# A planned decoder step on one core: samples' attention outputs taken by transposes and address patterns, value products in two row ranges, other planner constants

## The chip, the cores and the metric

The kernel runs on one core of a Trainium2 chip. The metric is the device time of one execution in microseconds. Three timed executions of the kernel before took 797.78, 797.87 and 798.31 us; their median is 797.87 us.

The core has five queues that run side by side: TensorE (PE in the profile; its weight loads are PEld), VectorE (DVE), ScalarE (ACT), GpSimd (POOL) and SyncE (SP), which here only issues transfers. Products land in PSUM, whose banks hold 512 float32 columns on 128 partitions; VectorE and ScalarE read them from there.

## The reference

One layer of a decoder computes a prompt of 512 tokens (`SEQ`) and 32 sample tokens (8 samples of 4 tokens, `NB`, `TS`, `NS`) with shared weights, all in float32. Cut to what matters here:

```python
h = rmsnorm(x, norm_mix)
z = h @ w_in                                  # aq, ak, av for 8 heads of 64; hq, hf, hi, hg for 4 heads of 128
att = dilated_attention(aq, k_all, v_all, q_idx)      # samples: k_all, v_all = cached window + new rows
att = head_rmsnorm(att, att_out_norm)
o, s_new = hgrn2_recurrence(...)
x = x + jnp.concatenate([att, o], axis=-1) @ w_out
c = rmsnorm(x, norm_cross)
cq = (c @ w_cq).reshape(B, T, X_H, X_DH)      # 4 heads of 128
s = jnp.einsum('bthd,bmhd->bhtm', cq, mem_k) * X_DH ** -0.5
co = jnp.einsum('bhtm,bmhd->bthd', softmax(s), mem_v)
x = x + co.reshape(B, T, X_W) @ w_co
x = x + (silu(conv(rmsnorm(x) @ w_gate)) * (rmsnorm(x) @ w_up)) @ w_down
```

For a sample, both attentions sum value rows that belong to that sample alone: the window attention over the cached rows and the four new tokens, the cross attention over 256 memory rows.

## The kernel before

Activations stand with features on the partitions (128 at a time) and the 544 tokens along the free dimension; the last 32 columns are the samples. Every large weight product is made of three products of split operands (`h` and `l` tiles: the rounded part, written by ScalarE, and the rest, written by VectorE). The input projection, the output projection `ps_wo`, the cross projections `ps_cq` and `ps_co`, and the feed-forward part (`ps_ag` to `ps_du`, then `ps_dz` and its like) follow one another. The samples' attention runs beside them.

**How samples are attended.** The scores of a sample need a query per head, so the queries are laid out as 32 columns per sample (8 heads x 4 tokens), each with zeros outside its own head. Four samples fill 128 rows of a score tile: row 32 b + 4 h + t belongs to sample b of the group, head h and token t. There are two such groups, `g` = 0 and 1. `decode_attention` computes the scores against the streamed key tiles (`psd`), applies the softmax, turns the probabilities by transposes (`psdt`), and multiplies them with the streamed value rows into `psdo`. That product makes for each of the 128 rows all 512 value features; a row of head h needs only the 64 features of its own head.

**How each row's own features are picked before.** `own_blocks` multiplies the product with `1 / den` (`dden`) and with a 0/1 mask `h8`, which zeroes the features of the other heads. `decode_finish` adds what the new tokens bring: per group four products of 32 x 32 probabilities (`pnew`) with the 32 new value rows (`vnew`), into `psdn`, masked in the same way (`domn`) and added to the masked `dom`. Then eight products with the 0/1 matrix `sel8` (128 x 16) sum over the heads' rows and at the same time turn the tile, so that features stand on partitions (`psds`). One copy takes that to `attS`, which is normalised, scaled and split into the tiles `am0h` to `am3l` that `ps_wo` reads. `cross_sample` does the same for cross attention with the mask `h4` (four heads of 128), the matrix `sel4`, and `ps_cos`, which `split_psum` turns into the last 32 columns of `coh` and `col`, read by the second halves of `ps_co`.

The new value rows come from `prompt_attention`: for each of four pairs of heads `by_token_s` multiplies the 32 sample columns of v with the identity into a spare corner of a score bank (32 rows x 128 columns), and a copy takes them to `vnew`.

**What sets the order.** The whole program is recorded first and put into an order by a planner, the class `Tape`. A call on an engine becomes a `Step`; neighbouring calls of one engine become one step (`tape.cut()` ends it). TensorE steps recorded inside `tape.main()` are *mains* and keep their order; all else is a *side*. `due` gives every side a time by which it should begin, worked back from the mains that use its result (`MARGIN` ahead of a main, `SLACK` where nothing presses). `order` then runs a simple model of the engines with a guessed length for each call and starts at every free engine the ready step that is due first, at most `LEAD` ahead of its time. For TensorE it collects ready sides until their lengths sum to `BURST`, or `PATIENCE` has gone by, or one is overdue, and then plays them in a run; a side of another array shape is put back by `NEAR`, and `SWITCH` is the modelled cost of a change of shape. `ACTIVE` and `SPELL` hold sides back that would leave too little matmul work in a spell of time. `run` first spreads the mains evenly over the total length of TensorE's steps, plans, moves each main's estimate 0.3 of the way to its planned start, and plans again, `ROUNDS` times; the plan with the earliest modelled end is issued. So every engine's program, the DMA queues' too, comes out of this plan; line 718 of the profile is where all recorded calls but the transfers (line 690) are issued.

Of the kernel before, what the change touches and what calls it, by code (L numbers as in the profile page):

```python
# [17 lines left out]
SEQ = 512  # L18
# [77 lines left out]
for _n, _c in (("ident", 128), ("ones", 128), ("blk64", 128), ("dbias", NR + 2 * NS),  # L96
               ("mask_a", 96), ("mask_b", 96), ("mask_s", 96), ("batch", 4), ("h8", 8), ("h4", 4), ("sel8", 16),
               ("sel4", 16), ("sel32", 32), ("own", 2)):
    _span(CST_COLS, _n, _c)
# [17 lines left out]
def _constants():  # L117
# [39 lines left out]
    put("h8", (h[:, None] == np.arange(8)[None, :]).astype(np.float32))  # L157
    put("h4", (h[:, None] == np.arange(4)[None, :]).astype(np.float32))
    bt = (p // 32) * TS + t
    put("sel8", (bt[:, None] == np.arange(16)[None, :]).astype(np.float32))  # L160
    put("sel32", (p[:, None] % 32 == np.arange(32)[None, :]).astype(np.float32))
    put("own", ((p[:, None] % 32) // TS == 4 * np.arange(2)[None, :] + p[:, None] // 32).astype(np.float32))
    put("sel4", ((bt[:, None] == np.arange(16)[None, :]) & (h[:, None] < 4)).astype(np.float32))
# [112 lines left out]
class Tape:  # L276
# [7 lines left out]
    ROUNDS = 6  # L284
    BLOCK, AHEAD_OF, FETCH = 256, 63, 4.3
    SWITCH, NEAR = 0.14, 3.0
    SPELL, ACTIVE, IDLE, COLD = 3.4, 0.47, 0.45, 2.0
    BURST, PATIENCE, SLACK, LEAD, MARGIN = 2.0, 4.0, 12.0, 15.0, 4.0
# [152 lines left out]
    def run(self):  # L441

        scale = sum(s.length for s in self.steps if s.engine == "PE") / sum(s.length for s in self.mains)
# [226 lines left out]
class _Engine:  # L670
# [5 lines left out]
    def __getattr__(self, method):  # L676
# [3 lines left out]
        def take(*args, **kw):  # L680
# [10 lines left out]
            if engine == "PE":  # L691
# [6 lines left out]
                else:  # L698
                    least = 0.112 if m == 128 and k == 128 else 0.0105
                    length = 2 * max(least, 0.00086 * n * (max(m, 128 - 2 * k) / 128 if m < 128 else 1.0) * (0.59 if k <= 64 else 1.0))  # L700
                work = n * (1 if method != "transpose" and args[1].dtype == F32R else codes) / 2400.0 * m * k / 16384
# [21 lines left out]
def tile_decoder_step(ctx: ExitStack, tc: tile.TileContext, xT, memT, kwT, vw, s0, conv_in, mkT, mv, vecs, cst,  # L723
# [497 lines left out]
    vnew, vnew_in = tape.tile(strm, [NS, 512], F32, name="vnew"), []  # L1221
# [18 lines left out]
    def decode_attention():  # L1240
# [36 lines left out]
        for g in range(2):  # L1277
            s = dec_p[g]
            pts = []
            for half in range(2):  # L1280
                pt = A(f"dpt{g}{half}")
                ps = PX(f"psdt{g}{half}")
                for c in range(4):
# [3 lines left out]
                    else:  # L1287
                        nc.tensor.transpose(ps[:NS, 128 * c:128 * c + 128], s[:, NR:NR + NS], C("ident"))
                if half == 0:
                    nc.scalar.copy(pt[:, :512], ps)  # L1290
                else:
                    nc.scalar.copy(pt[:, :384], ps[:, :384])
                    nc.scalar.copy(pt[:NS, 384:512], ps[:NS, 384:512])
# [11 lines left out]
            own_blocks(om_old[g], po, g)  # L1305
            nc.vector.tensor_copy(pnew[g], pts[1][:NS, 384:512])
# [5 lines left out]
    pnew = [tape.tile(strm, [NS, 128], F32, name=f"pnew{g}") for g in range(2)]  # L1312
# [3 lines left out]
    def own_blocks(out, ps, g):  # L1316
# [1513 lines left out]
```

## Time and profile before

| what | us |
|---|---|
| median of three timed executions | 797.87 |
| span of the profiled execution, first to last instruction | 796.6 |
| TensorE busy, matmuls | 784.4 (98%) |
| VectorE busy | 674.9 (85%) |
| ScalarE busy | 481.0 (60%) |
| GpSimd busy | 200.6 (25%) |
| TensorE busy, weight loads (beside matmuls) | 743.1 (93%) |

The profiled execution has no device time of its own beside the span; the timed executions lie 1.2 to 1.7 us above the span. Matmuls overlap in the records (a matmul starts before the one ahead of it ends), so what a group costs is the distance between its first start and the first start behind it. One float32 product makes two matmul records, a split product of two `h` or `l` tiles one, and a transpose one. The form `128*32` means 128 rows and 32 columns of the array.

### The profile page before, as it was taken

The page shows a single profiled execution, that of the slowest core. Times are in us where ns is not written, and L with a number is a line of the kernel's source. Part 1 is how long each engine was busy: PE and PEld are TensorE (multiplying, and loading weights), DVE is VectorE, ACT ScalarE, POOL GpSimd, SP SyncE. Part 2 cuts the span into 40 slices and gives each one's busy share as a digit, 9 for nine tenths or more (in the row PEclk, how much of TensorE's full clock was granted, in tenths as well). Part 3 has the DMA queues.
Part 4 walks back from the last instruction along what each step waited for, and adds up shares of the span by engine and source line. Part 5 has one row for each costly group of instructions (what it writes and reads, how often), then busy time and mean ns, then how long its engine had stood idle before and what let it go on. Part 6 is the DMA issues. An engine that isn't in the chain of part 4 may idle for free.

```text
span 796.6 us, 19239 instructions
## 1 busy us (share of the span) xinstructions
PE 784.4 (98%) x7448; PEld 743.1 (93%) x7448; DVE 674.9 (85%) x1515; ACT 481.0 (60%) x1031; POOL 200.6 (25%) x284
## 2 busy tenths in 40 slices
PE   9999999999999999999999999999999999999995
PEld 8999878988888989999999999999999999999994
DVE  6899888587979996674888999999998998979973
ACT  7734468726558535553666678666766666668642
POOL 1130000020220200231234346423533352332023
PEclk9999999999999999999999999999999999999998
DMA  8845795798932455450853368879788878776203
GB/s 303 264 147 163 249 337 191 246 357 286 296 109 80 135 173 196 132 173 26 255 156 95 91 171 193 167 189 205 165 175 206 198 150 208 186 202 168 78 1 112
DMA packets 107419, 144.14 MB, mean 181 GB/s; under 512 B 7360, under 2 KB 73920, under 8 KB 107328
## 3 DMA queue, kind: packets, MB, share of 16 engines
q1 hardware_dynamic: 91728, 124.04, 48.6%
q0 software_dynamic: 14880, 18.36, 15.1%
q8 instruction: 58, 0.95, 0.5%
q10 hardware_dynamic: 720, 0.53, 0.2%
q14 instruction: 33, 0.27, 0.1%
HBM read 134.82 MB, written 8.07 MB: 179 GB/s over the span
## 4 chain that ended last, share of the span: by engine, by line
PE 96%; ACT 1%; DMA 1%; DVE 0%; issue 0%; SPq 0%; DVEq 0%; ACTq 0%
PE ps_ag L718 7%; PE ps_au L718 7%; PE ps_wo L718 6%; PE ps_aw L718 5%; PE ps_cu L718 4%; PE ps_cg L718 4%; PE ps_q L718 3%; PE ps_co L718 3%; PE ps_cq L718 3%; PE ps_dz L718 3%; PE ps_az L718 3%; PE ps_hv L718 2%; PE ps_cw L718 2%; PE ps_first L718 2%; PE ps_ck L718 2%; PE ps_dg L718 2%
## 5 line engine op out<-in xcount | busy, mean ns | idle before, releaser
L718 DVE TENSOR_TENSOR wl<-wr,wh 128x512 fp32r<-128x512 f32 x98 | 70.8, 743 | 0.4 <-ACT wh L718 0.4
L718 ACT CAST wh<-wr 128x512 fp32r<-128x512 f32 x98 | 56.2, 616 | 15.2 <-PE psdo L718 6.0
L718 POOL TENSOR_TENSOR hG<-hG,hf 128x256 f32<-128x256 f32 (+1 forms) x28 | 23.8, 851 | 133.9 <-DVE hf L718 79.7
L718 POOL COPY last<-ug 128x2 f32<-128x2 f32 (+1 forms) x44 | 30.4, 726 | 85.2 <-DVE ug L718 79.3
L718 DVE SCALAR_TENSOR_TENSOR cv<-ug,vec,cv 128x560 f32<-128x560 f32 x44 | 35.1, 797 | 2.6 <-ACT cv L718 2.2
L718 POOL TENSOR_TENSOR acc_cx<-acc_cx,sq_cx 128x256 f32<-128x256 f32 (+1 forms) x14 | 12.3, 879 | 63.4 <-PE ps_wo L718 36.7
L718 ACT ACTIVATE cv<-cv 128x560 f32<-128x560 f32 x22 | 14.8, 672 | 13.4 <-DVE cv L718 13.3
L718 ACT ACTIVATE cv<-ug,vec 128x560 f32<-128x560 f32 x22 | 18.8, 856 | 4.6 <-DVE ug L718 2.1
L718 POOL COPY ug<-conv_state 128x16 f32<-128x16 f32 x22 | 20.7, 945 | 0.1
L718 ACT ACTIVATE P<-P,mx 128x128 f32<-128x128 f32 (+3 forms) x32 | 17.6, 552 | 4.0 <-DVE mx L718 3.8
L690 POOL DMA_DIRECT2D S13w<-in_w_down x12 | 12.2, 1019 | 30.7 <-PE ps_cw L718 15.8
L718 PE MATMUL ps_co<-coh,wh 128*128 128x256 f32 (+1 forms) x64 | 19.0, 297 | 0.0
L718 PE MATMUL ps_co<-col,wh 128*128 128x256 f32 (+1 forms) x64 | 18.4, 288 | 0.0
L718 PE MATMUL ps_co<-coh,wl 128*128 128x256 f32 (+1 forms) x64 | 18.4, 287 | 0.0
L718 DVE TENSOR_TENSOR xr<-xr,ps_wo 128x256 f32<-128x256 f32 (+1 forms) x16 | 6.8, 435 | 13.0 <-PE ps_wo L718 12.9
L718 ACT COPY keptg<-ps_ag 128x272 f32<-128x272 f32 x20 | 7.7, 387 | 15.7 <-PE ps_ag L718 15.7
L718 POOL TENSOR_TENSOR acc_final<-acc_final,sq_final 128x256 f32<-128x256 f32 (+1 forms) x10 | 8.5, 859 | 34.1 <-ACT sq_final L718 20.5
L718 DVE TENSOR_TENSOR xr<-xr,ps_aw 128x272 f32<-128x272 f32 x36 | 15.5, 431 | 0.6 <-PE ps_aw L718 0.6
L718 DVE CUSTOM_DVE_ANT_0 P<-psS,bias 128x128 f32<-128x128 f32 (+3 forms) x32 | 14.1, 486 | 1.9 <-PE psS L718 1.8
L718 PE MATMUL psd<-st,qbd_win 128*32 128x224 f32 x256 | 15.5, 357 | 0.0
L718 PE MATMUL psdo<-st,dpt 128*32 128x256 f32 x224 | 15.3, 384 | 0.0
L718 POOL TENSOR_TENSOR acc_ux<-acc_ux,sq_ux 128x256 f32<-128x256 f32 (+1 forms) x13 | 10.9, 839 | 16.4 <-ACT sq_ux L718 16.4
(3348 smaller groups left out, 3785.6 us busy)
## 6 DMA issues: line engine op xcount, KB each, us to landing
st<-in_kwT SPq DMA_DIRECT2D x32, 448.0 KB, 5.6
st<-in_vw SPq DMA_DIRECT2D x28, 512.0 KB, 6.2
wr<-in_w_in SPq DMA_DIRECT2D x25, 512.0 KB, 6.0
wrg<-in_w_gate SPq DMA_DIRECT2D x10, 512.0 KB, 6.4
wru<-in_w_up SPq DMA_DIRECT2D x10, 512.0 KB, 5.8
st<-in_mkT SPq DMA_DIRECT2D x8, 512.0 KB, 6.2
wr<-in_w_out SPq DMA_DIRECT2D x8, 512.0 KB, 4.5
S13w<-in_w_down SPq DMA_DIRECT2D x24, 128.0 KB, 3.5
```

Of the source, the lines that this page charges most:

```text
L690: return tape.put(engine, lambda: call(*args, **kw), outs, ins, 0.1, 0.3, size)
L718: return tape.put(engine, lambda: call(*args, **kw), outs, ins, length, lag, size, port, codes, work, mode)
```

## The change

1. The masks `h8`, `h4` and the matrices `sel8`, `sel4` are gone from the constants. `psdo` is taken to `dom` by ScalarE with the scale `dden`, unmasked; `ps_cso` to `com` by a plain ScalarE copy.
2. `by_feature` turns a whole 128 x 512 tile by four transposes, and `own_columns` is an address pattern over the result that reads, for head h, sample b and token t, column 32 b + 4 h + t of the block in which head h's features lie. ScalarE copies by that pattern: for the window attention one copy per group and half of the partitions (64 features per head), to `attS`; for cross attention one per group, to a new tile `cos`, from which `split_psum` reads.
3. `pnew` is one tile of 64 rows and `vnew` has 64 rows, with the new value rows twice (`by_token_s` runs for both row ranges). Group 1's products use rows 32 to 63. The last score block of group 1 is transposed as 64 columns, so that its 32 new columns land in rows 32 to 63, and ScalarE writes them to `pnew` directly. The products of both groups are recorded one after another; then comes for each group one VectorE pass (`psdn` times `dden` plus `dom`), a cut, the transposes and the copies.
4. The planner: other values, a factor `EVEN` on the first spread of the mains, two rounds instead of six, and half the modelled length for products of at most 32 rows and 32 columns.

```diff
-    ROUNDS = 6
+    ROUNDS, EVEN = 2, 1.013
     BLOCK, AHEAD_OF, FETCH = 256, 63, 4.3
-    SWITCH, NEAR = 0.14, 3.0
-    SPELL, ACTIVE, IDLE, COLD = 3.4, 0.47, 0.45, 2.0
-    BURST, PATIENCE, SLACK, LEAD, MARGIN = 2.0, 4.0, 12.0, 15.0, 4.0
+    SWITCH, NEAR = 0.14, 3.9
+    SPELL, ACTIVE, IDLE, COLD = 3.4, 0.45, 0.45, 2.0
+    BURST, PATIENCE, SLACK, LEAD, MARGIN = 1.75, 3.7, 16.5, 15.95, 4.95
...
-        scale = sum(s.length for s in self.steps if s.engine == "PE") / sum(s.length for s in self.mains)
+        scale = self.EVEN * sum(s.length for s in self.steps if s.engine == "PE") / sum(s.length for s in self.mains)
...
+                    length *= 0.5 if k <= 32 and m <= 32 else 1.0
...
-    vnew, vnew_in = tape.tile(strm, [NS, 512], F32, name="vnew"), []
+    vnew, vnew_in = tape.tile(strm, [2 * NS, 512], F32, name="vnew"), []
...
-                        nc.tensor.transpose(ps[:NS, 128 * c:128 * c + 128], s[:, NR:NR + NS], C("ident"))
+                        nc.tensor.transpose(ps[:NS + NS * g, 128 * c:128 * c + 128], s[:, NR - NS * g:NR + NS], C("ident"))
...
-                    nc.scalar.copy(pt[:NS, 384:512], ps[:NS, 384:512])
+                    nc.scalar.copy(pnew[own, :], ps[own, 384:512])
...
-            own_blocks(om_old[g], po, g)
-            nc.vector.tensor_copy(pnew[g], pts[1][:NS, 384:512])
+            nc.scalar.activation(om_old[g][:, :512], po, AF.Copy, scale=dden[g])
...
+    def new_rows(g):
+        return slice(NS * g, NS * g + NS)
+
+    def own_columns(ps, rows, first, step, count):
+
+        of = ps[rows, :]
+        return bass.AP(of.tensor, of.offset + first, [list(of.ap[0]), [128 + step, count], [32, 4], [1, TS]])
+
+    def by_feature(om, name):
+
+        ps = PX(name)
+        for c in range(4):
+            nc.tensor.transpose(ps[:, 128 * c:128 * c + 128], om[:, 128 * c:128 * c + 128], C("ident"))
+        return ps
 
     def decode_finish(out):
 
-        oms = []
+        pos = [(PX if g else PDEC)(f"psdn{g}") for g in range(2)]
         for g in range(2):
-            po = (PX if g else PDEC)(f"psdn{g}")
+            rows = new_rows(g)
             for b in range(4):
-                nc.tensor.matmul(po[32 * b:32 * b + 32, :], pnew[g][:, 32 * b:32 * b + 32], vnew, start=True, stop=True)
+                nc.tensor.matmul(pos[g][32 * b:32 * b + 32, :], pnew[rows, 32 * b:32 * b + 32], vnew[rows, :],
+                                 start=True, stop=True)
+        for g in range(2):
             om = A(f"domn{g}")
-            own_blocks(om, po, g)
-            nc.vector.tensor_tensor(om[:, :512], om[:, :512], om_old[g][:, :512], op=ALU.add)
-            oms.append(om)
-        px = PX("psds")
-        for g in range(2):
-            for p in range(4):
-                at = slice(32 * p + 16 * g, 32 * p + 16 * g + 16)
-                nc.tensor.matmul(px[:, at], oms[g][:, 128 * p:128 * p + 128], C("sel8"), start=True, stop=True)
-        nc.scalar.copy(attS, px[:, :128].rearrange("p (q n) -> p q n", q=4))
+            nc.vector.scalar_tensor_tensor(om[:, :512], pos[g], dden[g], om_old[g][:, :512], op0=ALU.mult, op1=ALU.add)
+            tape.cut()
+            px = by_feature(om, f"psds{g}")
+            for hh in range(2):
+                rows = slice(64 * hh, 64 * hh + 64)
+                nc.scalar.copy(attS[rows, :, 16 * g:16 * g + 16].rearrange("p q (b t) -> p q b t", t=TS),
+                               own_columns(px, rows, 4 * hh, 8, 4))
...
-                spare = S[group, 1][:NS, 384:512]
-                by_token_s(v, spare)
+                spare = S[group, 1][:2 * NS, 384:512]
+                for g in range(2):
+                    by_token_s(v, spare[new_rows(g), :])
...
-            nc.vector.tensor_tensor(om[:, :512].rearrange("p (h d) -> p h d", h=4),
-                                    po.rearrange("p (h d) -> p h d", h=4),
-                                    C("h4")[:, :, None].to_broadcast([128, 4, 128]), op=ALU.mult)
+            nc.scalar.copy(om[:, :512], po)
             oms.append(om)
-        pcs = PX("ps_cos")
+        cos = A("cos")[:, :128].rearrange("p (h n) -> p h n", h=XH)
         for g in range(2):
-            for h in range(XH):
-                at = 32 * h + 16 * g
-                nc.tensor.matmul(pcs[:, at:at + 16], oms[g][:, 128 * h:128 * h + 128], C("sel4"), start=True,
-                                 stop=True)
+            pcs = by_feature(oms[g], f"ps_cos{g}")
+            nc.scalar.copy(cos[:, :, 16 * g:16 * g + 16].rearrange("p h (b t) -> p h b t", t=TS),
+                           own_columns(pcs, slice(0, 128), 0, 4, XH))
         for h in range(XH):
-            split_psum(h, pcs[:, 32 * h:32 * h + 32], SEQ, N)
+            split_psum(h, cos[:, h, :], SEQ, N)
```

More of the change, by code (lines that the diff above doesn't have):

```diff
@@ L96 @@
 for _n, _c in (("ident", 128), ("ones", 128), ("blk64", 128), ("dbias", NR + 2 * NS),
-               ("mask_a", 96), ("mask_b", 96), ("mask_s", 96), ("batch", 4), ("h8", 8), ("h4", 4), ("sel8", 16),
-               ("sel4", 16), ("sel32", 32), ("own", 2)):
+               ("mask_a", 96), ("mask_b", 96), ("mask_s", 96), ("batch", 4), ("sel32", 32), ("own", 2)):
     _span(CST_COLS, _n, _c)
@@ L156, in _constants @@
     put("batch", ((p[:64, None] % 32 // TS) == 4 * (p[:64, None] // 32) + np.arange(4)[None, :]).astype(np.float32))
[L157 to L160, printed above, removed]
     put("sel32", (p[:, None] % 32 == np.arange(32)[None, :]).astype(np.float32))
     put("own", ((p[:, None] % 32) // TS == 4 * np.arange(2)[None, :] + p[:, None] // 32).astype(np.float32))
-    put("sel4", ((bt[:, None] == np.arange(16)[None, :]) & (h[:, None] < 4)).astype(np.float32))
     return c
@@ L1291, in decode_attention @@
                 else:
+                    own = new_rows(g)
                     nc.scalar.copy(pt[:, :384], ps[:, :384])
-                    nc.scalar.copy(pt[:NS, 384:512], ps[:NS, 384:512])
+                    nc.scalar.copy(pnew[own, :], ps[own, 384:512])
                 pts.append(pt)
@@ L1311, in tile_decoder_step @@
     om_old = [A(f"dom{g}") for g in range(2)]
-    pnew = [tape.tile(strm, [NS, 128], F32, name=f"pnew{g}") for g in range(2)]
+    pnew = tape.tile(strm, [2 * NS, 128], F32, name="pnew")
     dden = [tape.tile(strm, [128, 1], F32, name=f"drec{g}") for g in range(2)]
     attS = tape.tile(strm, [128, 4, NS], F32, name="attS")
-    def own_blocks(out, ps, g):
-        nc.vector.scalar_tensor_tensor(out[:, :512].rearrange("p (h d) -> p h d", h=8),
-                                       ps.rearrange("p (h d) -> p h d", h=8), dden[g],
-                                       C("h8")[:, :, None].to_broadcast([128, 8, 64]), op0=ALU.mult, op1=ALU.mult)
+    def new_rows(g):
+        return slice(NS * g, NS * g + NS)
```

## The prediction

> **What bounds the kernel now.** I read the page first: the engine totals and the chain that ended last.
>
> ```profile
> span 796.6 us, 19239 instructions
> ...
> PE 784.4 (98%) x7448; PEld 743.1 (93%) x7448; DVE 674.9 (85%) x1515; ACT 481.0 (60%) x1031; POOL 200.6 (25%) x284
> ...
> PE 96%; ACT 1%; DMA 1%; DVE 0%; issue 0%; SPq 0%; DVEq 0%; ACTq 0%
> ```
>
> TensorE is busy for 784.4 of 796.6 us and 96% of the last-ending chain runs through it. A busy share can hide gaps, so next come the busy times by stage, and then what TensorE waited for between the start and the end (9 to 787 us). Columns of the first: the stretch, its length, TensorE's busy time and matmuls, granted clock, DMA share, GB/s.
>
> ```profile
> 160.00:306.30 146.30, 146.30 (x1876) 1.00 0.64 206
> 430.00:730.00 300.00, 299.07 (x2383) 1.00 0.76 178
> 787.00:796.60 9.60, 0.70 (x2) 0.63 0.53 177
> ```
>
> ```profile
> PE ps_au L718 <- ACT keptu L718: 0.9, 1, 0.9
> PE ps_ak L718 <- ACT keptk L718: 0.5, 1, 0.5
> ```
>
> The stretch that holds the samples' attention (160 to 306 us) has no idle time on TensorE, and 300 us of feed-forward work have 0.9. In the middle only two waits are listed, 1.4 us together. So a matmul stream's microsecond is a microsecond of the kernel until something else ends last, and work taken from VectorE or ScalarE alone buys nothing. I cost the change by the time that it takes from or adds to TensorE's stream, from one start to the next (durations overlap, starts do not).
>
> **The change part by part.** *Selection by a mask product becomes selection by address.* Before, two groups of eight 128x16 products with the 0/1 matrices sel8 and sel4 pick each sample's own rows; after, two sets of four 128x128 transposes do it per place, and ScalarE reads only the wanted columns. The TensorE timeline shows both products and, as nearest row for the new form, four transposes between dense matmuls (start, duration, operation).
>
> ```profile
> 296.19 1.86 PE L718 MATMUL psds<-cs,domn 128*128 128x16 f32 x16
> 297.89 0.38 PE L718 MATMUL psr_hg<-hsh,sums 128*128 128x288 f32 x1
> ...
> 411.04 1.85 PE L718 MATMUL ps_cos<-cs,com 128*128 128x16 f32 x16
> 412.74 0.36 PE L718 MATMUL ps_co<-coh,wh 128*128 128x256 f32 x1
> 412.94 0.28 PE L718 MATMUL ps_co<-col,wh 128*128 128x256 f32 x1
> ...
> 379.77 0.60 PE L718 MATMUL ps_cpt<-cs,cp 128*128 128x128 f32 x4
> 380.12 0.36 PE L718 MATMUL ps_cpo<-cpth,mvh 128*128 128x256 f32 x1
> 380.32 0.28 PE L718 MATMUL ps_cpo<-cptl,mvh 128*128 128x256 f32 x1
> 380.44 0.28 PE L718 MATMUL ps_cpo<-cpth,mvl 128*128 128x256 f32 x1
> ...
> 283.95 0.60 PE L718 MATMUL pst_hk<-cs,hk 128*128 128x128 f32 x4
> 284.48 0.41 PE L718 MATMUL psL<-kq 128*32 128x32 f32 x13
> ```
>
> Each product holds TensorE 1.70 us (297.89 - 296.19; 412.74 - 411.04): sixteen records for eight matmuls. Four transposes hold it 0.35 us (380.12 - 379.77). The first dense matmul behind either takes 0.20 instead of 0.12 (380.32 - 380.12 against 380.44 - 380.32; 412.94 - 412.74 is 0.20 too), so splitting a place into two sets costs 0.08 once more. After: 2 x 0.35 + 0.08 = 0.78 per place, saving 1.70 - 0.78 = 0.92, twice, 1.84 us. Bounds: a set that is followed by another array shape holds it 0.53 (284.48 - 283.95); were all four sets so placed, a place would save 1.70 - 1.06 = 0.64, 1.3 in all. Eight transposes in one set save the 0.08 at most.
>
> *New tokens' value products in two row ranges.* pnew and vnew get 64 rows, and the second group of samples works in rows 32 to 63, so that its four 32x32 products can run beside those of the first; both groups become one step.
>
> ```profile
> 276.13 1.06 PE L718 MATMUL psdn<-vnew,pnew 32*32 32x512 f32 x8
> 277.13 1.09 PE L718 MATMUL psO<-PT,vt 128*64 128x128 f32 x16
> ...
> 285.67 1.06 PE L718 MATMUL psdn<-vnew,pnew 32*32 32x512 f32 x8
> 286.66 1.16 PE L718 MATMUL psU<-hvt,hkt 128*128 128x128 f32 x8
> ...
> 288.33 1.13 PE L718 MATMUL psu<-hvm,hsm 32*128 32x512 f32 x4
> 289.38 0.50 PE L718 MATMUL ps_cv<-wh,mmh 128*128 128x512 f32 x1
> ```
>
> Today the two groups hold TensorE 1.00 and 0.99 us, each alone. That row groups overlap here is seen in psu: two 32-row products of 512 columns, in different row groups, take 1.05 us together, as long as four column groups of psdn. I take 1.05 for all eight: saving 1.99 - 1.05 = 0.94. If the second group's first pass starts only with the first group's second pass, they take about 1.5 and save 0.5; with no overlap 0. I take the first, since psu is the nearest row.
> The Trainium skill ("TensorE: Matmul & The Clock Gate", Part 3, what overlaps) says that matmuls start and end strictly in program order; if each product's two passes stood next to each other in that order, the halfway case would hold, 0.44 us less gain. psu's 1.05 us speaks against it, since one such product after another would show more.
>
> *By-token copies of the new values.* by_token_s runs twice, into rows 0 to 31 and 32 to 63, four times in all. The nearest row has two such products of hv side by side:
>
> ```profile
> 275.79 0.41 PE L718 MATMUL psA<-cs,hv 128*32 128x128 f32 x4
> ```
>
> Four records hold TensorE 0.34 us (276.13 - 275.79), about three 0.11 steps for two products; were the added one free, two records would take about the same. I charge 0.03 each, 0.1 in all; were they serial, four pairs of 0.11 passes, 0.9.
> Sum on TensorE: 1.84 + 0.94 - 0.1 = **2.7 us less**, between 0.4 (1.3 + 0 - 0.9) and 2.8.
>
> *VectorE and ScalarE.* The groups by form (busy us, mean ns of one), and from the timeline the one small copy of today:
>
> ```profile
> L718 DVE SCALAR_TENSOR_TENSOR dom<-psdo,drec,cs 128x512 f32<-128x512 f32 x2 | 1.5, 746 | 0.9 <-PE ps_hg L718 0.9
> L718 DVE TENSOR_TENSOR com<-ps_cso,cs 128x512 f32<-128x512 f32 x2 | 1.4, 688 | 0.0
> L718 DVE TENSOR_TENSOR domn<-domn,dom 128x512 f32<-128x512 f32 x2 | 1.3, 686 | 0.0
> L718 ACT ACTIVATE P<-P,den 128x512 f32<-128x512 f32 x4 | 2.8, 721 | 2.1 <-DVE den L718 2.1
> L718 ACT COPY dpt<-psdt 128x512 f32<-128x512 f32 x2 | 1.2, 581 | 0.0
> ...
> 298.08 0.27 ACT L718 COPY attS<-psds 128x128 f32<-128x128 f32 x1 [2.49 <-PE psds L718]
> ```
>
> VectorE loses dom, com and one of the two domn passes, 1.5 + 1.4 + 1.3 = 4.2 us, and two small pnew copies. ScalarE gains two scaled evacuations (nearest: 721 ns), two plain ones (581 ns), and five more small strided copies; at 0.27 us each, as today's attS copy (0.58, the 512-column copy, would be the most), about 1.4 + 1.2 + 1.4 = 4.0 us. Both lie beside TensorE work and I cost them at nothing. The cover is the dense work behind the two places:
>
> ```profile
> 303.42 0.25 DVE L718 SCALAR_TENSOR_TENSOR am3l<-attS,vec,am3h 128x32 fp32r<-128x32 f32 x1
> 307.16 0.28 PE L718 MATMUL ps_wo<-am0h,wh 128*128 128x256 f32 x1
> ...
> 413.50 0.47 DVE L718 TENSOR_TENSOR col<-ps_cos,coh 128x32 fp32r<-128x32 f32 x4
> 415.66 0.30 PE L718 MATMUL ps_co<-coh,wh 128*128 128x288 f32 x1
> ```
>
> attS's last part is ready at 303.67 and the output projection first reads an attention tile at 307.16: 3.5 us of slack, against three more small copies, 0.9. The cross path ends at 413.97 and its first reader starts at 415.66: 1.7 of slack, against two copies in a row, 0.6, less the 0.9 that TensorE needs less. If that cover went, the excess would be paid one for one; next late would be the second half of ps_co. Behind a new ScalarE evacuation that waits on psdo or ps_cso stand the wh casts for the next weights, which have a reader on VectorE (wl) before TensorE needs them; I see no stall of theirs on TensorE now. The constants h8, h4, sel8, sel4 leave the held table (44 columns), one load a little smaller: nothing. g = 1 transposes 64 columns instead of 32 of the last score block, the same instruction count: nothing.
>
> *Other constants of the recorder.* They change the order on all five queues, the loads on SP and POOL included, and two rounds of planning instead of six are compared. Matmul work does not change, so only waits and changes of array shape can move. The two waits above, 1.4 us, may go or double. A step between dense and small shapes costs about the 0.2 seen between a set and its neighbours; ten visits more or fewer, a choice of mine, are +-2 us. I see no sign either way and take 0, with bounds of -2.5 and +4.
>
> The sum is made against this execution, 796.6 of span: 796.6 - 2.7 = 793.9. Timed runs have a median of 797.87, 1.3 above the span, which is what lies around it; I keep that offset: 797.87 - 2.7 = **795.2 us**.
>
> **The rivals.** *The order gains too* (793.0): both waits go (1.4) and some four small-shape visits fewer (0.8): 795.2 - 2.2. For it: the wait for keptu is a queue effect; its copy starts at 726.05 behind other ScalarE work. Against it: no stage but these has idle time.
>
> ```profile
> 726.05 0.36 ACT L718 COPY keptu<-ps_au 128x272 f32<-128x272 f32 x1
> ```
>
> *The packing does not do what it says* (796.9): row groups run one after another (0.94 lost) and the doubled by_token_s is serial (0.8 lost): 795.2 + 1.7, no measurable change. psu and psA speak against it. *A clock window falls.* In the row 787 to 796.6 the clock is 0.63 where TensorE idles; a wait long enough would do that inside. Were 4 us of matmuls, a length that I choose, to run at 0.63, they would take 4 / 0.63 = 6.3: 795.2 + 2.3 = 797.5, still no measurable change. The stretch with most transposes now has 1.00.
> The Trainium skill ("TensorE: Matmul & The Clock Gate", Part 4) says that transposes do not count as activity for the clock; by that, the added transposes would feed this rival. The 1.00 in the stretch 160 to 306, which holds long sets of them, does not bear it out.
>
> *Slower: the feed-forward stream begins to wait for VectorE* (800.5).
>
> ```profile
> 457.50:560.00 102.50, 102.50 (x820) 102.50 (x819) 99.27 (x204) 70.51 (x146) 43.19 (x60) 1.00 0.79 184
> 560.00:650.00 90.00, 90.00 (x721) 90.00 (x721) 87.04 (x187) 58.00 (x121) 37.44 (x53) 1.00 0.83 184
> ```
>
> The third busy time is VectorE's: 99.27 of 102.50 and 87.04 of 90.00, 6.2 us free in all. New leads and margins order its casts anew; where a ready step is put behind one that waits, that reserve is used up, and each late evacuation then stops TensorE for about the 0.9 of keptu. Six such stops cost 5.3: 797.9 - 2.7 + 5.3. It decides from 4.3 us on (five stops). Against it: VectorE's load there does not change, and in 192 us TensorE never waited.
>
> **How the numbers follow.** A measurement tells some 0.2% (1.6 us) from no change: faster means under 796.3, slower over 799.5. The sum alone, 795.2 with 794.0 to 796.3 around it, 0.47; the order gains too 0.21; packing fails or the order takes the gain back, 0.17; clock 0.04; slower 0.11. Faster 0.68, same 0.21, slower 0.11. The range reaches from the order's bound (795.2 - 2.5) to the lower part of the slow case: 792.6 to 798.6.
>
> **What would show it.** psds and ps_cos as four transposes of 0.35 us each; psdn as one run of sixteen records in about 1.05 us; by_token_s pairs starting within 0.02 us; TensorE's busy time near 781.7 with the same few waits; clock 1.00 up to 787. Wrong would be: psdn near 2 us, waits of TensorE on VectorE or ScalarE summing to over 3 us between 430 and 730, a clock row under 1.00, or a first ps_wo or second-half ps_co that waits for attS or cos.

## The result and the profile after

The changed kernel is slower than the kernel before by a little: 799.49 us (median of 21 runs, 798.74 to 801.85) against 798.34 (21 runs, 797.73 to 799.63), a ratio of 1.0016 with a 95% interval of 1.0010 to 1.0023. Run again (e4 below) it gave 1.0017 (1.0008 to 1.0026). The prediction of 795.2, range 792.6 to 798.6, missed the time and the sign.

The page of the changed kernel gives its engine totals and the shares of the chain that ended last.

```profile
span 797.0 us, 19226 instructions
...
PE 784.1 (98%) x7440; PEld 742.0 (93%) x7440; DVE 673.9 (85%) x1507; ACT 480.1 (60%) x1040; POOL 206.6 (26%) x284
...
PE 97%; ACT 1%; DVE 1%; issue 0%; DVEq 0%; ACTq 0%
```

TensorE's busy time is 0.3 lower than before (784.4), where 2.7 were expected. So most of what is missing is not idle time: TensorE is busy longer with the products that did not change. The stretches of the changed kernel (length, TensorE's busy time and matmuls, granted clock, DMA share, GB/s) and TensorE's waits between 9 and 787 us follow.

```profile
160.00:306.90 146.90, 146.06 (x1870) 1.00 0.63 205
430.00:730.00 300.00, 299.02 (x2380) 1.00 0.75 179
```

```profile
PE ps_au L713 <- ACT keptu L713: 0.9, 1, 0.9
PE psds L713 <- ACT ho L713: 0.7, 1, 0.7
PE ps_ak L713 <- ACT keptk L713: 0.5, 1, 0.5
PE psA L713 <- issue: 0.2, 1, 0.2
```

The attention stretch, 146.3 of 146.3 busy before, now has 0.84 idle in 146.9, and of that 0.67 is one wait: the new transposes into psds wait for ScalarE's copy into ho. The clock is 1.00 in both. Next the rows of the changed products on TensorE (start, duration, operation).

```profile
275.28 1.09 PE L713 MATMUL psdn<-vnew,pnew 32*32 32x512 f32 x16
276.30 1.53 PE L713 MATMUL psO<-PT,vt 128*64 128x128 f32 x24
...
295.29 0.66 PE L713 MATMUL psds<-cs,domn 128*128 128x128 f32 x4 [0.67 <-ACT ho L713]
295.88 0.40 PE L713 MATMUL psin<-hsm 32*128 32x32 f32 x2
...
296.68 0.63 PE L713 MATMUL psds<-cs,domn 128*128 128x128 f32 x4
297.07 0.48 PE L713 MATMUL ps_cv<-wh,mmh 128*128 128x512 f32 x1
...
410.16 1.03 PE L713 MATMUL ps_cos<-cs,com 128*128 128x128 f32 x8
410.95 0.37 PE L713 MATMUL ps_co<-coh,wh 128*128 128x256 f32 x1
```

psdn holds TensorE 1.02 us for both groups (276.30 - 275.28), ps_cos 0.79 (410.95 - 410.16), psds 0.59 + 0.39 = 0.98, because psin stands between its two sets. So the products did become cheaper. To see where the time went instead, the table sets TensorE's first starts side by side: the first matmul of the samples' and prompt's mixing weights (ps_hv), of the output projection (ps_wo), of the feed-forward gate (ps_g), of the last down product (ps_dz), and the last matmul of all. Each column is the time between two of them, worked out from the starts in each trace. The labels are those of the experiments below; "after, again" is the second run of the changed kernel.

```
                                to ps_hv  ps_hv-ps_wo  ps_wo-ps_g  ps_g-ps_dz  ps_dz-last
before                             25.43       280.67      122.68      300.82       58.05
after                              24.96       281.78      121.67      301.19       58.11
after, again                       25.09       281.76      121.68      302.11       58.11
e1  new products, old constants    25.57       279.89      122.12      301.01       58.13
e2  old products, new constants    25.64       291.72      123.37      301.00       58.42
e3  before, NEAR 3.9               26.59       280.94      122.96      301.37       58.04
e5  after, psL copy first          24.70       280.90      121.67      302.54       58.11
e6  after, psds late               25.32       281.46      121.80      301.31       58.03
e7  after, moves of e5 and e6      26.41       281.12      121.81      302.12       58.02
e8  after, ug early                25.17       281.75      121.68      300.89       58.11
e9  after, four moves              26.97       280.65      121.81      301.26       57.97
e10 e1 with three moves            25.22       280.44      122.40      301.89       58.14
e11 before, ug late                25.12       280.68      122.68      303.09       58.05
e12 new products, old order        25.27       279.94      121.79      301.07       58.03
e13 e12 with keptu early           25.11       279.94      121.80      301.04       57.98
e14 e13 with domn early            26.62       279.11      121.69      300.72       58.02
```

The cross stage (ps_wo to ps_g) is 1.01 shorter, the 0.91 of ps_cos and a little more: there the prediction came true. The mixing stage (ps_hv to ps_wo) holds psdn, psds and by_token_s and should have lost 1.8; it is 1.11 longer. The feed-forward stage is 0.37 longer in one profile of the changed kernel and 1.29 in the other. Those two columns are what had to be explained.

### The profile page after: what moved, and what is told of

Same layout as the page of the kernel before. It is cut to its first block, busy times and chain, and to the rows that moved or that the text cites. A ratio compares the mean times of both kernels' runs of the same rounds, so it can differ in the third digit from the quotient of the medians.

```text
span 797.0 us, 19226 instructions
## 1 busy us (share of the span) xinstructions
PE 784.1 (98%) x7440; PEld 742.0 (93%) x7440; DVE 673.9 (85%) x1507; ACT 480.1 (60%) x1040; POOL 206.6 (26%) x284
## 4 chain that ended last, share of the span: by engine, by line
PE 97%; ACT 1%; DVE 1%; issue 0%; DVEq 0%; ACTq 0%
PE ps_ag L713 7%; PE ps_au L713 7%; PE ps_wo L713 6%; PE ps_aw L713 5%; PE ps_cu L713 4%; PE ps_cg L713 4%; PE ps_q L713 3%; PE ps_co L713 3%; PE ps_cq L713 3%; PE ps_first L713 3%; PE ps_dz L713 3%; PE ps_az L713 3%; PE ps_hv L713 2%; PE ps_cw L713 2%; PE ps_dg L713 2%; PE ps_ck L713 2%
## 5 line engine op out<-in xcount | busy, mean ns | idle before, releaser
L713 POOL COPY ug<-conv_state 128x16 f32<-128x16 f32 x22 | 17.9, 992 | 0.0
L713 POOL MEMSET hG<- 128x544 f32 x4 | 2.2, 550 | 56.0 <-PE psr_att L713 45.9
L713 DVE TENSOR_TENSOR hf<-hf 128x256 f32<-128x256 f32 (+1 forms) x28 | 12.2, 435 | 4.8 <-POOL hG L713 4.5
```

Source lines behind the costliest of these rows:

```text
L713: return tape.put(engine, lambda: call(*args, **kw), outs, ins, length, lag, size, port, codes, work, mode)
```

## The experiments

Except for e2, whose clock fell, all ran at a granted clock of 0.995 to 0.997. None leaves out any of the computation. Each ratio is to the kernel before, timed beside it.

**The two halves of the change apart, e1 and e2.** e1 is the changed kernel with the recorder's constants of before, e2 the kernel before with the new constants. The halved length for small products, which the change also brings, stays with e1 and is not in e2, so it is not taken apart from the products.

```diff
 # e1, in the changed kernel
-    ROUNDS, EVEN = 2, 1.013
+    ROUNDS, EVEN = 6, 1.0
-    SWITCH, NEAR = 0.14, 3.9
-    SPELL, ACTIVE, IDLE, COLD = 3.4, 0.45, 0.45, 2.0
-    BURST, PATIENCE, SLACK, LEAD, MARGIN = 1.75, 3.7, 16.5, 15.95, 4.95
+    SWITCH, NEAR = 0.14, 3.0
+    SPELL, ACTIVE, IDLE, COLD = 3.4, 0.47, 0.45, 2.0
+    BURST, PATIENCE, SLACK, LEAD, MARGIN = 2.0, 4.0, 12.0, 15.0, 4.0
```

> The changed kernel with the recorder's constants of before (ROUNDS 6, no EVEN, NEAR 3.0, ACTIVE 0.47, BURST 2.0, PATIENCE 4.0, SLACK 12, LEAD 15, MARGIN 4). If the constants' order eats the saving (theory 1), this one keeps it: about 2.3 us under the kernel before (796.0), with the transposes and the packed products as short as in the changed kernel. If the new structure itself makes the waits, by its second bank for the transposes (theory 2), it is as slow as the changed kernel: 799.5, with a wait of some 0.8 us in front of the first psds. If every new order moves waits by chance (theory 3), anything from 795 to 800, with waits at other places.

> The kernel before with only the recorder's new constants. Theory 1: slower by what the saving was eaten by, 2.3 + 1.2 = 3.5 us, so about 801.8. Theory 2: no change, 798.3. Theory 3: anywhere within some 3 us of before, with waits of its own that the changed kernel doesn't have.

> The kernel before with one constant alone changed, NEAR 3.0 to 3.9 as in the change. Theory 1 makes no claim on one constant; if it were this one, 801. Theory 2: 798.3. Theory 3: the order differs in most of the first 430 us and the time by some 1 to 3 us in either direction, though the matmul work is the same.

e1 took 797.47 us (796.48 to 799.32), ratio 0.9991 (0.9982 to 1.0000); e2 810.88, ratio 1.0159 (1.0145 to 1.0173); e3, where only NEAR went from 3.0 to 3.9, 799.15 (798.56 to 800.65), ratio 1.0012 (1.0003 to 1.0021). The new constants cost 2.0 us with the new products and 12.5 with the old ones, so there is no price of the constants as such: each combination gets its own order, and with it its own waits. Stretches of e2 with the waits of its TensorE:

```profile
100.00:160.00 60.00, 59.73 (x624) 1.00 0.80 266
160.00:317.00 157.00, 150.95 (x1875) 0.97 0.59 193
```

```profile
PE ps_ck L718 <- DVE v L718: 2.7, 1, 2.7
PE psS L718 <- DVE hst L718: 1.4, 1, 1.4
...
PE psin L718 <- DVE hin L718: 0.9, 1, 0.9
```

The 11 us that its mixing stage lost are 6.05 of idle time, and a clock of 0.97 where every other kernel had 1.00. The clock falls right behind the two longest waits, 1.4 us before 272.2 and 2.7 us before 275.8: it is 0.65 from 272 to 276 and 0.50 from 276 to 280, though TensorE is busy all through the second stretch. e1 fell between its two theories: new products under old constants do gain, but 0.9 and not 2.4.

**Two waits behind a PSUM bank, e4 to e7.** The new order of the changed kernel has two stalls in the mixing stage that the order before had not. One is the wait of psds above. The other shows in no list of waits, but in a duration: the scores psS of two heads, four passes in two groups of 64 rows. First the row of the kernel before, then the changed kernel's, with ScalarE's rows around it.

```profile
187.42 1.13 PE L718 MATMUL psS<-k,q 64*128 64x512 f32 x4
```

```profile
189.77 1.28 ACT L713 ACT_TABLE_LOAD   x1
191.07 0.36 ACT L713 COPY hAT<-psL 64x256 f32<-64x256 f32 x1
...
190.93 1.68 PE L713 MATMUL psS<-k,q 64*128 64x512 f32 x4
```

The second head's psS is put into the bank from which ScalarE still copies psL, and that copy stands behind three sigmoids and a table load. Its first pass starts at 191.49, when the copy is done (191.07 + 0.36); the two heads, which run side by side in 1.13 before, run one behind the other in 1.68. Both stalls come from the same place in the recorder: it counts free banks of the pool that psS, psds, psdn and ps_cos share, but which bank a tile gets is decided by the pool's own turn. e5 issues the copy hAT<-psL ahead of the sigmoid step, e6 issues the first transposes into psds behind psin, e7 does both; e4 is the changed kernel itself beside them.

```diff
 # in Tape.run, before the steps are issued; late and ahead are steps of the plan
+        plan.remove(late)                        # e5: last hAT1 <- psL1 on ACT
+        plan.insert(plan.index(ahead), late)     #     ahead of hqs2, hgs2 on ACT
+        plan.remove(late)                        # e6: psds0 on PE
+        plan.insert(plan.index(ahead) + 1, late) #     behind hin3, psin3 on PE
```

> The changed kernel itself, timed beside the next three. Theory (a late bank): of the 2.7 us that the products' terms promised, about 2 went into two places where TensorE waits because the new tile stands in a PSUM bank that ScalarE is still reading, psS behind psL's last copy and psds behind pso's. Rival (order as a whole): the new order costs a little everywhere, and these two waits are only where it shows. Both expect 799.5 here, between 798.7 and 801.9, ratio to before 1.0005 to 1.003.

> After, with the one ScalarE copy hAT<-psL that holds psS's bank issued ahead of the joined sigmoid step and its table load instead of behind it; nothing else moves. Late-bank theory: the two psS products run side by side, 0.53 us of start-to-start per pair less twice over, so 1.06 us less on TensorE and 0.997 to 0.999 of the changed kernel: 798.4. Rival: the wait goes to the next tile that ScalarE owes (the sigmoids' readers come 0.36 us later) and the time stays at 799.5, within 0.4.

> After, with the transposes into psds0 issued behind the psin step on TensorE instead of ahead of it; nothing else moves. Late-bank theory: the wait of 0.7 for ho's copy of pso, which holds psds0's bank, is covered by psin's work; 0.7 to 0.84 us less: 798.7. Rival: the wait is only passed on, since psin then waits for its own operand or attS comes later for the output projection (3.5 us of slack in the kernel before): 799.5, within 0.4.

> After, with both of the last two moves. Late-bank theory: the two add up, 1.8 to 1.9 us less than the changed kernel: 797.6, which is also 0.7 under the kernel before. Rival (order as a whole): 799.0 to 799.5. In between (one move helps, the other not): 798.5.

e4 took 799.98 us, ratio 1.0017 (1.0008 to 1.0026); e5 799.47, 1.0011 (1.0002 to 1.0019); e6 799.50, 1.0015 (1.0006 to 1.0023); e7 799.27, 1.0009 (1.0000 to 1.0018). Both stalls were gone from the traces in which they had been moved. The first row is e5's psS pair, again 1.13 long; then comes TensorE's longest wait in e5.

```profile
190.34 1.13 PE L722 MATMUL psS<-k,q 64*128 64x512 f32 x4
...
PE ps_aw L722 <- DVE xr L722: 1.4, 1, 1.4
```

Of the 1.9 that the theory promised, the median fell by 0.7 at most, and the intervals overlap. The stage table shows less than was promised in the mixing stage too: against e4 it is 0.86 shorter in e5 (1.06 promised), 0.30 in e6 (0.7 to 0.84) and 0.64 in e7 (1.8). The psS steps fell by 0.55, since one pair had lost its overlap and the expectation counted it twice; in e6, 0.43 of what the transposes gained came back at ps_cv behind them, 0.24 of it as a new wait of psr_attS for ScalarE. And e5 gave back half of its gain behind ps_g, where its stage is 302.54 against e4's 302.11. So the two stalls are real, and the theory that they took about 2 us is not borne out.

**A late copy on GpSimd, e8 and e11.** The wait for xr is in e4 too (1.0), and not in the first profile of the changed kernel, which is one of its quickest runs: it comes in some executions and not in others. (In that first profile ScalarE's cv waits 1.1 for the same copy, and TensorE does not.) The chain of waits of e4 at that place, in order of time (start, duration, what):

```profile
493.99 1.71 POOL S1u L684
495.70 2.86 POOL ug L713 x2
...
498.59 0.02 ACT cv L713
...
499.35 0.41 ACT wTh L713
...
499.79 0.03 DVE wTl L713
...
501.18 0.41 DVE up L713 x2
501.60 0.34 DVE xr L713
501.94 0.70 DVE wXl L713 x2
502.64 0.36 DVE xr L713
...
503.14 0.99 PE ps_aw L713 x6
```

GpSimd copies 16 columns of the convolution's state into ug; ScalarE's cv reads them, and behind cv in ScalarE's queue stands the cast wTh that VectorE's wTl needs; behind wTl stand the xr passes that free ps_aw's bank. In the kernel before, that copy stood ahead of three weight loads on GpSimd's queue and was done at 490.3 for a reader at 496.1; the new order puts it behind them, at 494 to 498. e8 moves it back in the changed kernel, e11 moves it late in the kernel before; nothing else changes its place among its neighbours.

```diff
+        for s in late:                              # e8: conv_state -> ug5 and its memset on POOL,
+            plan.remove(s)                          #     ahead of the load A22w0_0l on POOL;
+            plan.insert(plan.index(ahead), s)       # e11: S1u6's load, then these, just ahead of cv5 on ACT
```

> After, with GpSimd's copy of the convolution state into ug (tile 5) and its memset issued ahead of three weight loads on GpSimd's queue instead of behind them; nothing else moves. New theory (late GpSimd copy): in most executions of the changed kernel the copy ends late, ScalarE's cv waits 1.9 for it, VectorE's wTl 1.3 for ScalarE, and TensorE's ps_aw 1.0 near 502 us; with the copy early this wait is gone in every run, so the median falls from 799.7 to about 798.8 and the spread of the runs from 3 us to about 1.5, as before's. Rival (the start scatters): the runs differ by when the first loads land, before 25 us, and median and spread stay at 799.5 to 800 and 3 us.

> The kernel before, with the copy of the convolution state into ug (tile 5) and its memset issued behind the same three weight loads on GpSimd's queue as in the changed kernel; nothing else moves. Late-copy theory: the wait near 502 us appears here too, in most runs: 0.5 to 1.2 us more than before, 798.9 to 799.6, with runs up to 801. Rival (start scatter, or the rest of the new order): unchanged, 798.4 within 0.3, no longer tail.

e8 took 798.69 us (798.34 to 800.21), ratio 1.0009 (1.0000 to 1.0018): a median 1.3 under e4's (0.6 by the ratios), a spread of 1.9 for 3.1. In its trace cv does not wait for ug, ps_aw does not wait, and the feed-forward stage is 1.2 shorter than e4's and 0.3 shorter than in the first profile. By the ratios alone, whose intervals overlap with e4's, the gain would not be settled, and three of its eleven runs still took 800.0 to 800.2. e11 shows from the other side that such a late copy costs time: 800.67 (800.37 to 802.37, 5 runs), ratio 1.0034 (1.0021 to 1.0046), 2.4 over the kernel before and twice what was expected, and its feed-forward stage is 2.3 longer. A scatter of the start does not explain that; it stays true that the start scatters as well. But the link is another one than in the changed kernel: in the order of before, ScalarE's copy into ps_dw stands behind cv, and TensorE waits 2.0 for that copy. So e11 shows the mechanism, and its 2.4 is not the price in the changed kernel, which is put at 0.6 to 1.3 by e8. GpSimd's rows in e8, then from e11 the waits of ScalarE and TensorE, and ScalarE's copy:

```profile
489.77 0.78 POOL L724 COPY ug<-conv_state 128x16 f32<-128x16 f32 x1
490.48 0.10 POOL L724 MEMSET ug<- 128x2 f32 x1
492.53 1.20 POOL L695 DMA_DIRECT2D A22w_0l<-in_w_down  x1 [1.96 <-ACT A22w_0l L724]
```

```profile
ACT cv L729 <- POOL ug L729: 2.4, 1, 2.4
...
PE ps_dw L729 <- ACT ps_dw L729: 2.0, 1, 2.0
...
499.04 0.38 ACT L729 COPY ps_dw<-ps_aw 128x272 f32<-128x272 f32 x1
```

**All waits that were found, e9 and e10.** e9 is the changed kernel with the moves of e5, e6 and e8, and with the copy keptu<-ps_au near 726 us issued ahead of ScalarE's cv step. e10 takes e1, moves keptu likewise, both sets of psds behind one more block of ps_cv, and psr_attS and psr_hg behind another.

```diff
+        plan.remove(late)                        # last keptu20 <- ps_au20 on ACT
+        plan.insert(plan.index(ahead), late)     # ahead of cv21 <- ug21 on ACT
```

> After, with both bank moves, the early copy into ug, and the copy keptu<-ps_au near 726 us issued ahead of ScalarE's cv step. If waits of TensorE explain the lost saving, they add: 799.7 - 1.06 (psS) - 0.75 (psds) - 0.9 (ps_aw) - 0.45 (keptu) = 796.5, ratio to before 0.9975. If the moves only shift waits, as the two bank moves did when together they gave 0.7 of 1.9: 798 to 799.

> After's structure with before's constants (797.5 when it ran alone, profiled span 795.7), with two moves of issue order: both transposes into psds behind one more block of ps_cv, the sums psr_attS and psr_hg behind another, and keptu<-ps_au near 725 us ahead of ScalarE's cv step. If its waits come off one for one: 0.4 (psds) + 0.45 (keptu) less, 796.6, ratio to before 0.998. Rival (only shifted): 797.5 within 0.3.

e9 took 797.81 us (797.34 to 799.67), ratio 0.9994 (0.9985 to 1.0002): 1.9 under the 799.7 from which its expectation counted (2.2 under e4's median), where the four moves were to give 3.2. e10 took 797.63, ratio 0.9993 (0.9985 to 1.0002), nothing over e1: its trace has lost the wait of psds and half of keptu's 0.9, and has a new one, of the sums psr_att; its mixing stage is 0.55 longer than e1's.

```profile
PE psr_att L729 <- ACT rh_att L729: 1.1, 1, 1.1
...
PE ps_au L729 <- ACT keptu L729: 0.5, 1, 0.5
```

In e9 no wait of over 0.5 was left on TensorE, and the mixing stage was as long as that of the kernel before (280.65 and 280.67), though its own products were 1.8 cheaper. Either the rest was the order, in changes of shape and short stalls that no list names, or the new products have a price of their own in any order.

**The new products in the old order, e12 to e14.** e12 takes the changed kernel and issues its steps in the order of the kernel before, on every engine: each step is looked up by its engine and the tiles that it touches, and the few new ones stand where those that they replace stood. e13 adds the move of keptu, e14 also puts VectorE's second domn pass directly behind the first.

```diff
+        for s in self.steps:
+            name = s.engine, tuple(sorted(t.rsplit("_", 1)[0] for t in s.tiles))
+            found = sorted(places[key(*STANDS_FOR.get(name, name))])
+            n = met[name] = met.get(name, -1) + 1
+            s.place = found[min(n, len(found) - 1)][1], s.number
+        plan, left = [], sorted(self.steps, key=lambda s: s.place)
...
 # e14, in STANDS_FOR: the place of domn1 <- psdn1
-    ('DVE', ('dom1', 'domn1')),
+    ('DVE', ('cs2', 'domn1', 'drec1', 'psdn1')),
```

> The products and copies of the changed kernel, issued in the order of the kernel before on every engine: each step that both kernels have stands where it stood before; the changed steps stand where those that they replace stood (both psdn groups at the place of the second group, both sets of transposes at that of the mask products, the copies of ScalarE where the passes of VectorE stood). Theory (the order took the saving): the 2.4 of the products (0.96 + 0.91 + 0.88, less 0.29 for by_token_s) come off the time of before in full: 795.9, ratio to before 0.997; the waits psS, psds and ps_aw of the changed kernel are absent. Rival (the products give back what they save through their own followers and a second PSUM bank, in any order): 797.5 to 798.3, as the changed structure gave with the constants of before, 797.5.

> The same as the run before it, with the copy keptu<-ps_au near 726 us issued ahead of the cv step of ScalarE, whose wait of 0.9 every kernel so far has shown. In two kernels this move left a wait of 0.5 in its place, so 0.4 less than the run before it: 795.5, ratio to before 0.9965, if the saving of the products arrives; if the later start of cv is passed on to VectorE and back to TensorE (a wait of 0.2 of ps_cu on up was seen), the same time as the run before it, within 0.2.

> The run before it (new products, old order, keptu early), with the second domn pass of VectorE directly behind the first, ahead of hin and a weight cast instead of behind them: it ends 0.9 earlier and frees the PSUM bank for which the first pso product waits 0.67 in the last two runs. Theory (what is left over from the products is this wait for the second bank): 0.67 less, 796.0, ratio to before 0.9972, and the wait pso on domn is gone from the trace. Rival (the cast that now comes 0.7 later is missed in its turn): 796.6 within 0.2, with a wait of ps_cv for wl.

e12 took 796.76 us (796.46 to 798.58), ratio 0.9985 (0.9976 to 0.9994); e13 796.64, ratio 0.9981 (0.9972 to 0.9990); e14 **795.64** (794.91 to 796.91, 6 runs), ratio **0.9965** (0.9953 to 0.9977). e12 gave 1.5 of the 2.4. Its TensorE rows and waits show all terms and what was missing:

```profile
284.53 1.09 PE L1023 MATMUL psdn<-vnew,pnew 32*32 32x512 f32 x16
285.55 1.16 PE L1023 MATMUL psU<-hvt,hkt 128*128 128x128 f32 x8
...
290.59 0.68 PE L1023 MATMUL pso<-hAT,hvt 128*128 128x128 f32 x4 [0.67 <-DVE domn L1023]
...
296.00 1.04 PE L1023 MATMUL psds<-cs,domn 128*128 128x128 f32 x8
296.80 0.38 PE L1023 MATMUL psr_hg<-hsh,sums 128*128 128x288 f32 x1
```

psdn takes 1.02 and psds, its eight transposes in one run, 0.80. The stalls of psS, psds and ps_aw are absent, as the theory had it. What is new is a wait of 0.67 of pso for VectorE's second domn pass: both groups of psdn are now written in one step, so their second bank is held longer, and pso was to have it. e14 frees it 0.9 earlier; the wait is gone (its list follows) and the median falls by 1.0, of which 0.67 were expected; between the two traces the mixing stage falls by 0.83.

```profile
PE psr_mix L1031 <- DVE acc_mix L1031: 0.7, 1, 0.7
PE psr_final L1031 <- ACT sq_last L1031: 0.5, 1, 0.5
PE ps_ak L1031 <- ACT keptk L1031: 0.5, 1, 0.5
PE ps_au L1031 <- ACT keptu L1031: 0.5, 1, 0.5
PE ps_cu L1031 <- DVE up L1031: 0.2, 1, 0.2
```

In the stage table e14's mixing stage is 1.56 and its cross stage 0.99 shorter than before, 2.55 together, which is also what the medians differ by (798.19 - 795.64). Its profiled run is its slowest, at 796.91: the first ps_hv came 1.2 later than in the profile of before. e12 and e13 beat both kernels too, by less; e14 is the quickest of all.

## Why the prediction was wrong, step by step

**Products: right.** The sets of transposes were predicted at 0.78 a place and measure 0.79 (ps_cos of the changed kernel) and 0.80 (psds in e12); only psds in the changed kernel takes 0.98, with psin between its sets. psdn was predicted at 1.05 and measures 1.02 in both. The halfway case of about 1.5 did not come. The Trainium skill ("TensorE: Matmul & The Clock Gate", Part 3, what overlaps) has matmuls start and end strictly in program order, which would have given the halfway case if each product's two passes were neighbours. The trace shows that they are not: the eight first passes of psdn start between 275.28 and 275.33 and the eight second ones between 275.73 and 275.78, so the choice of psu as the nearest row was sound. by_token_s was charged 0.1: TensorE's steps at these products sum to 0.85 before, 0.91 in e12, and 1.14 in the changed kernel, in whose order three of the four visits stand alone, where only one did before. In the old order the sum of 2.7 stands at 0.96 + 0.91 + 0.91 - 0.06 = 2.72.

**VectorE and ScalarE at nothing: right, in the sense in which it was said.** No kernel shows a wait of ps_wo for attS, nor of ps_co for cos. But the cover was looked for in engines alone. The edits also ask for PSUM banks: psds and ps_cos want two where they wanted one, and psdn holds its two at once. No term of the sum named a bank. This cost 0.67 at psds in the new order and 0.67 at pso in the old one, until a single VectorE pass moved.

**"I see no sign either way and take 0": the step that failed.** The term for the new order was put at nothing, and it is what took the saving. The order of the changed kernel costs 799.49 - 796.76 = 2.7 us against the same products in the order of before, and 3.9 against e14, which has two moves more. (Of the 4.3 by which the time was missed, 0.5 is the base: the kernel before has a median of 798.34 over 21 runs, where the prediction had 797.87 from three.) The term was inside the bounds that the text gave (-2.5 and +4), but the range was not carried to them: 795.2 + 4 is 799.2, and the range ended at 798.6. At the other end 795.2 - 2.5 is 792.7 and not 792.6, which changes nothing.

The text named waits and changes of array shape as all that an order can move. It can also move overlap: TensorE's busy time was to fall by 2.7 and fell by 0.3. How wide the term is was not in the profile of one order: e3, with one constant changed and no product, lost 0.8, e1 1.6 of the products' 2.5, the changed kernel 3.7 to 4 (1.2 or 1.55 over before, and the 2.5), e2 12.5. All four lost; none gained.

Of the changed kernel's 2.7 to 3.9, the runs name about 0.55 (psS behind psL), 0.7 (psds behind pso, of which moving it gave back 0.3) and about 1 (the copy into ug; 0.9 between the feed-forward stages of the changed kernel's two profiles). The rest, 1.5 in the mixing stage (280.65 in e9 for 279.11 in e14), is spread over many groups. Summed from one start to the next, psS takes 0.90 more in e9 than in e14 (0.67 at its score products, which stand in ten runs of neighbouring steps where they stood in eight, and 0.23 at by_token_s), pst_v 0.40, ps_cv 0.36 (with that wait of psr_attS) and psd 0.29 more, psA 0.44, psT 0.31 and psO 0.30 less. No run took this apart, and it stays open which of these matter and why.

**The rivals.** The order did not gain. Packing did not fail. The clock stayed at 1.00 in the changed kernel; that a bad order can lower it is seen in e2's 0.97. In e2 it does so behind waits of 1.4 and 2.7 us, as the clock rival had it. The slower rival came near the time (800.5 for 799.49 to 799.98) partly by luck: TensorE did wait for VectorE in the feed-forward stage, but about 1 us, and most of the loss lies in the mixing stage, which that rival does not name. Nor is its mechanism, six late evacuations because VectorE's reserve is used up, what happened. It is one wait, and VectorE itself waits, for ScalarE, which waits for GpSimd. The sentence against it, that TensorE never waited in 192 us, said how full the queues were and nothing of how near to late each hand-over was.

**What would show it.** The product readings came out nearly as listed: psdn and ps_cos did, psds came in two sets of 0.59 and 0.39, and three of the four pairs of by_token_s start within 0.02 us, one within 0.04. TensorE's busy time was to be near 781.7 and is 784.1, and the waits were to stay the same few; a reader with this list would have looked at the psds wait first, and would still have missed psS, which lengthens a busy row, and the copy into ug, for which TensorE does not wait in this one profile.

## What to carry to other kernels

A cheaper operation is worth its time only in an order that stays put: when an edit also makes a planner order everything anew, take the order's effect as a term with its own sign and size, and measure the two apart by issuing the new work in the old order. Cost the buffers that an edit asks for (here PSUM banks) as carefully as its instructions. For each engine that only prepares things, compare when its result is done with when it is read, since a hand-over with 6 us to spare and one with none look the same in every busy share.

## What was not expected of the hardware

Two products in different row groups (each on its own rows of the array) lost their overlap when only the second one waited at its first pass: the psS pair takes 1.68 for 1.13, and 1.13 again in e5, while the list of waits shows nothing, since TensorE counts as busy.

The same GpSimd copy, 128 by 16 elements, takes 0.67 us in one place (at 489.66 in the kernel before) and 3.98 in another (rows of VectorE in e4, then of GpSimd):

```profile
497.80 0.68 DVE L713 TENSOR_TENSOR S13w_0l<-S13w,S13w_0h 128x512 fp32r<-128x512 f32 x1
499.79 0.44 DVE L713 TENSOR_TENSOR wTl<-wT,wTh 128x272 fp32r<-128x272 f32 x1 [1.30 <-ACT wTh L713]
...
494.54 3.98 POOL L713 COPY ug<-conv_state 128x16 f32<-128x16 f32 x1
495.56 3.13 POOL L713 COPY ug<-conv_state 128x16 f32<-128x16 f32 x1
```

1.16 of the 3.98 are the load's issue still running (until 495.70 in the chain). The copy ends at 498.52, right behind VectorE's pass S13w_0l, which ends at 498.48. That is no accident of this trace: of the 352 copies into ug in the 16 traces 112 took 1 us or more, and 103 of these end 0.03 to 0.07 us behind the end of a VectorE pass, where a tenth of all moments lie so. In e4 VectorE then has nothing to do, since it waits for what hangs on this copy; in the kernel before, e6 and e8 it goes straight on with its next pass. The Trainium skill ("SBUF — State Buffer", SBUF: two separate sides) says that a VectorE pass with two SBUF inputs and a GpSimd operation that reads SBUF, as this copy does, share a pair of ports as an exclusive lock, which the first to start holds for its whole instruction. The trace agrees with that for passes like S13w_0l. In e6, e8 and e9 the copy also ends 0.03 behind a pass with one input in PSUM (up<-ps_cu,keptu), which that rule does not name. No run here took VectorE's passes away, so the lock as the cause is argued and not shown.

The start scatters too: the first ps_hv came between 24.70 and 26.97 us in these profiles, with the same loads in the same order in several of them.
